# R times the state, for both scan directions, in one group over four quarters of the array

## The chip, the core and the metric

The kernel runs on one core of a Trainium2 chip. The metric is the device time of one launch in microseconds (us). Engines are named as in the profile: PE is TensorE's matmuls, PEld its weight loads, DVE VectorE, ACT ScalarE, POOL GpSimd, and SPq the queue of SyncE, which issues the DMAs.

## What is computed

A two-layer backbone over 1024 latent tokens and 256 context tokens of width 1024. Layer 0 mixes tokens with a bidirectional RWKV-7 scan, layer 1 with a Fourier transform; a squared-ReLU MLP follows each. What the change touches is the scan's output: per direction and head (16 heads of 64), a state S is carried through the tokens and read by r.

```
def step(s, inp):                                  # one token; inp = w, k, v, a, b, r
    sa = einsum('bhvk,bhk->bhv', s, a)
    s  = s * w[:, :, None, :] + sa[..., None] * b[:, :, None, :] + v[..., None] * k[:, :, None, :]
    y  = einsum('bhvk,bhk->bhv', s, r)
    return s, y
# for each direction: context tokens first (no y), then latent tokens from that state;
# direction 1 runs over the tokens in reverse
out = readout(y_direction0 + y_direction1)
```

## The kernel before

**Chunks.** The scan runs in 20 steps of 64 tokens (`scan_step`, line 912, called with i = 0 to 19): four context steps, then sixteen latent steps with outputs (`lat`). Each step handles a chunk of direction 0 and one of direction 1 (loop variable `d`). Within a chunk the recurrence is turned into matrix products, by head; a tile of 128 partitions holds two halves of 64 (`hh`), and `q` counts eight pairs of heads. `HR` names the two halves in order, `OR` the same two swapped.

**Products of one step.** Scores between the chunk's tokens (L957) go to banks 0 to 3 and give L (whose columns from `C` on hold r) and l2. `scan_invert` (line 1069) inverts the triangular part for both directions at once: L1147, L1160, L1183 and L1192 are 32-row products on TensorE, with transposes on VectorE between them; L1136 turns the keys. Then, for each direction, a chain: `x_mm` (L1014), a copy, `u_mm` (L1023), two copies of U into `sv`, and `s_mm` (L1037), which gives the next state. With outputs, `r_mm` (L1053) multiplies r with the state `st` and `y_mm` (L1059) adds l2 times `sv` in the same PSUM bank Y; ScalarE copies Y to `y` (L1065), and SP stores it to `s_y` (issued by the helper `dma`, L922). x, U, s and Y share three PSUM banks, 5 to 7 (`CHAIN`). In `r_mm` the half hh of L and of `st` lies on partitions `HR[hh]` and the output goes to partitions `HR[hh]` of Y, so one group uses the two quarters of 64x64 on the diagonal of the 128x128 array. The code's 16 float32 matmuls of a group stand as 32 rows in the profile.

**Rings.** Tiles come in turn from fixed places (`SCAN_RINGS`, line 278): six for L (three steps of two), three for `sv`, two each for `st`, `t` and `y`.

**The order.** Each operation is entered in a list (`plan.add`) with its engine, a planned duration, the keys it reads and writes, its bank and a `load` (how dense its TensorE work is counted). `Plan.emit` (line 165) then runs a list scheduler over all of it: it books each operation at its planned time, longest remaining path first, hands out banks and ring places, and writes the order of every engine's queue, SP's included, before anything runs. At run time each queue is strictly in its written order.

**Readout.** `readout` (line 1298) loads `s_y` of both directions by 128 tokens, adds them and goes on; the keys `("sy", d, chunk)` hold its loads (L1264) back until the stores are done. Behind it only matmuls with their epilogues follow: L368 to L370 are the three products in which a float32 product is split.

Of the kernel before, what the change touches and what calls it, by code (L numbers as in the profile page):

```python
# [22 lines left out]
CTX = 256  # L23
# [3 lines left out]
C = 64  # L27
# [264 lines left out]
SCORES, INVERT, CHAIN = range(4), (4,), range(5, 8)  # L292
# [38 lines left out]
class Kernel:  # L331
# [545 lines left out]
    def slot(self, name):  # L877
        k = self.count.get(name, 0)
        self.count[name] = k + 1
        ring = self.rings[name]  # L880
        return ring[k % len(ring)], (name, k % len(ring))
# [30 lines left out]
    def scan_step(self, i):  # L912
        nc, plan, slot = self.nc, self.plan, self.slot
        lat = i >= CTX // C
# [3 lines left out]
        HR = [slice(hh * 64, hh * 64 + 64) for hh in range(2)]  # L918
        OR = [HR[1], HR[0]]

        def dma(dst, src, kb, r=(), w=(), eng="q"):
            return plan.add(eng, min(1.3, kb / 200.0), lambda: nc.sync.dma_start(dst, src), r, w, hold=0.7)  # L922


        S = []
        for d in range(2):
            lo = i * C if d == 0 else (T + CTX - (i + 1) * C if lat else CTX - (i + 1) * C)
            c = 2 if not lat else (lo - CTX) // 512
            L, kL = slot("L")
            bk, kb = slot("bk")  # L930
            E = dict(lo=lo, c=c, L=L, kL=kL, bk=bk, kb=kb)
# [10 lines left out]
        for d in range(2):  # L942
            E = S[d]
            L, kL, bk, kb = E["L"], E["kL"], E["bk"], E["kb"]
            l2, k2 = slot("l2")
            bkt, kt_ = slot("bkt")
            E.update(l2=l2, k2=k2, bkt=bkt, kt=kt_)
            for h4 in range(2):
# [13 lines left out]
                for hh, B in enumerate(BB):  # L962
                    rs, ro = HR[hh], OR[hh]
                    bv = lambda B=B: B.tile.rearrange("p (q t) -> p q t", q=4)
                    ys = slice(d * 8 + q4.start, d * 8 + q4.stop)
# [18 lines left out]
        for d in range(2):  # L984
            E = S[d]
            sv, kv = slot("sv")
# [17 lines left out]
        for d in range(2):  # L1004
            E = S[d]
            L, kL, sv, kv = E["L"], E["kL"], E["sv"], E["kv"]
            lall = [(kL, "a", 0), (kL, "a", 1)] + [(kL, "k", hh, h4) for hh in range(2) for h4 in range(2)]
            vall = [(kv, z, hh) for z in ("s", "v") for hh in range(2)]
            B, U = self.plan.bank(CHAIN), self.plan.bank(CHAIN)

            def x_mm(B=B, L=L, sv=sv):
                for q in range(8):
                    for hh in range(2):
                        nc.tensor.matmul(B.tile[HR[hh], q * C : (q + 1) * C], L[hh][:, q, 0:C], sv[:, hh, q, :], start=True, stop=True)  # L1014

            self.at = plan.add("pe", 1.1, x_mm, lall + vall, [B], B, load=0.95)
            xs, kx = slot("xs")
            plan.flex({"act": 0.58}, lambda e, B=B, xs=xs: self.copy_on(e, xs, B.tile), [B], [kx], B)

            def u_mm(xs=xs, d=d, U=U):  # L1020
                for q in range(8):
                    for rs in HR:
                        nc.tensor.matmul(U.tile[rs, q * C : (q + 1) * C], tt[rs, d * 8 + q, :], xs[rs, q * C : (q + 1) * C],  # L1023
                                         start=True, stop=True)

            plan.add("pe", 1.1, u_mm, [kx, *kT], [U], U, load=0.5)
            for hh in range(2):
                plan.flex({"act": 0.58, "dve": 0.69}, lambda e, sv=sv, hh=hh, U=U: self.copy_on(
                    e, sv[HR[hh], hh].rearrange("p q c -> p (q c)"), U.tile[HR[hh]]), [U], [(kv, "s", hh)], U)
            if i < NCH - 1:  # L1030
                bkt, kt_ = E["bkt"], E["kt"]
                B = self.plan.bank(CHAIN)

                def s_mm(B=B, bkt=bkt, sv=sv):
                    for q in range(8):
                        for hh in range(2):
                            nc.tensor.matmul(B.tile[HR[hh], q * C : (q + 1) * C], bkt[:, hh, q, :], sv[:, hh, q, :],  # L1037
                                             start=True, stop=True)

                t, kt0 = slot("t")  # L1040
                plan.add("pe", 1.2, s_mm, vall + [(kt_, 0), (kt_, 1)], [B, kt0], B, load=0.78)
                self.state[d] = (t, kt0, [("pcs", d, kt, E["c"]) for kt in range(KT)])
                plan.add("dve", 0.68, lambda B=B, t=t, st=E["st"]: nc.vector.tensor_tensor(
                    t, B.tile.rearrange("p (q v) -> p q v", q=8), st, ALU.add), [B, E["ks"]], [kt0], B)
            if lat:
                l2, k2 = E["l2"], E["k2"]

                Y = self.plan.bank(CHAIN)

                def r_mm(B=Y, L=L, st=E["st"]):  # L1050
                    for q in range(8):
                        for hh in range(2):
                            nc.tensor.matmul(B.tile[HR[hh], q * C : (q + 1) * C], L[hh][HR[hh], q, C:], st[HR[hh], q, :],  # L1053
                                             start=q == 0, stop=False)

                def y_mm(B=Y, l2=l2, sv=sv):
                    for q in range(8):
                        for hh in range(2):
                            nc.tensor.matmul(B.tile[HR[hh], q * C : (q + 1) * C], l2[:, q, hh, :], sv[:, hh, q, :],  # L1059
                                             start=False, stop=q == 7)  # L1060

                plan.add("pe", 1.15, r_mm, vall + [E["ks"], (kL, "a", 0), (kL, "a", 1)], [Y], Y, load=0.5)
                plan.add("pe", 1.15, y_mm, vall + [(k2, hh, h4) for hh in range(2) for h4 in range(2)], [Y], Y, load=1.0)
                y, ky = slot("y")
                plan.add("act", 0.58, lambda B=Y, y=y: nc.scalar.copy(y, B.tile), [Y], [ky], Y)  # L1065
                dma(self.s_y[d, E["lo"] - CTX : E["lo"] - CTX + C].rearrange("t (h c) -> h t c", h=2), y, 256, [ky],
                    [("sy", d, (E["lo"] - CTX) // C)])

    def scan_invert(self, mab, kM, S):

# [227 lines left out]
    def readout(self):  # L1298
# [4 lines left out]
        def unit(t, qh):  # L1303

            ts_ = slice(t * P, (t + 1) * P)
            hq = lambda a: a.rearrange("p (h q c) -> p h q c", h=2, q=4)
            qv = lambda a: a.rearrange("p (q h c) -> p h q c", h=2, q=4)
            ys = [[("sy", d, 2 * t + z) for z in range(2)] for d in range(2)]
            y0, y1, v = [self.raw(src.rearrange("t (h x) -> t h x", h=2)[:, :, qh * 256 : qh * 256 + 256], 256,
                                  lambda t: t.rearrange("p (h x) -> p h x", h=2), r)  # L1310
                         for src, r in ((self.s_y[0, ts_], ys[0]), (self.s_y[1, ts_], ys[1]),
                                        (self.s_v[CTX + t * P : CTX + (t + 1) * P], [("v", qh, 2 + t)]))]
            m = self.M()
            plan.flex({"dve": 0.6, "pool": 1.24}, lambda e: self.engines[e].tensor_tensor(y0.tile, y0.tile, y1.tile, ALU.add),
                      [y1], [y0])
            plan.add("dve", 0.6, lambda: nc.vector.tensor_reduce(m.tile[:, 0:8], hv(y0.tile), AX.X, ALU.add), [y0], [m])
            plan.add("dve", 0.65, lambda: nc.vector.scalar_tensor_tensor(
                hv(y0.tile), bc(m.tile[:, 0:8]), -1.0 / C, hv(y0.tile), ALU.mult, ALU.add), [m], [y0])
            plan.add("act", 0.53, lambda: nc.scalar.activation(y1.tile, y0.tile, AF.Square), [y0], [y1])
            plan.add("dve", 0.6, lambda: nc.vector.tensor_reduce(m.tile[:, 8:16], hv(y1.tile), AX.X, ALU.add), [y1], [m])  # L1320
            plan.add("act", 0.25, lambda: nc.scalar.activation(
                m.tile[:, 16:24], m.tile[:, 8:16], AF.Sqrt, bias=self.eps[:, 1:2], scale=1.0 / C), (), [m])
            plan.add("dve", 0.1, lambda: nc.vector.reciprocal(m.tile[:, 24:32], m.tile[:, 16:24]), (), [m])
            ya, vb = self.S(), self.S()
            plan.flex({"dve": 0.6, "pool": 1.24}, lambda e: self.engines[e].tensor_tensor(
                qv(ya.tile[:, :512]), hq(y0.tile), m.tile[:, 24:32].rearrange("p (h q e) -> p h q e", h=2, e=1).broadcast_to(
                    [P, 2, 4, C]), ALU.mult), [y0, m], [ya])
            plan.flex({"dve": 0.6, "pool": 1.24}, lambda e: self.engines[e].tensor_tensor(
                qv(vb.tile[:, :512]), hq(v.tile), self.bon[:, t, qh * 8 : qh * 8 + 8].rearrange(
                    "p (q h e) -> p h q e", h=2, e=1).broadcast_to([P, 2, 4, C]), ALU.mult), [v, *[("bon", 4 * qh + k, t // 4) for k in range(4)]], [vb])  # L1330
            return ya, vb
# [631 lines left out]
```

## Time and profile before

| | |
|---|---|
| median of 3 runs | 3021.74 us (3017.54 to 3023.11) |
| profiled execution | 3018.24 us, its span 3016.5 us |
| mean granted clock of TensorE | 0.947 |
| TensorE busy (PE) | 2820.9 us, 94% of the span |
| weight loads (PEld) | 2187.5 us, 73% |
| VectorE busy | 1883.4 us, 62% |
| ScalarE busy | 997.1 us, 33% |
| GpSimd busy | 496.4 us, 16% |

A share is an average over the whole span, and stages differ; what a change in one stage is worth is read from that stage. "Idle before <-X" is time in which the engine stood still ahead of an instruction, put down to X, whose result came last; "issue" is idle time for which no wait shows. Matmuls overlap, so the start of one group and that of the next tell more than the length of one matmul.

### The profile page before, as it was taken

Reading aid. Unit: us, or ns where it says so; the run is one execution under the profiler, and the core shown is the slowest. Engines: PE = TensorE matmul, PEld = TensorE weight load, DVE = VectorE, ACT = ScalarE, POOL = GpSimd, SP = SyncE. Lnnn points to the kernel's source line nnn. Section 1 sums busy time; section 2 is a strip of 40 time slices with the busy share of each in tenths; the row PEclk is TensorE's granted clock in tenths of the full one; section 3 lists DMA queues with packets and bytes.
Section 4 is the critical chain, followed back from the end, with each engine's and each line's share of the span. In section 5 each row is a group of like instructions: output and inputs, shape, how many; then the busy total and the mean of one; then the engine's idle time right before and its main releaser. Section 6 shows DMA issues by size and latency. Waiting matters only on the chain.

```text
span 3016.5 us, 63005 instructions
## 1 busy us (share of the span) xinstructions
PE 2820.9 (94%) x26640; PEld 2187.5 (73%) x26640; DVE 1883.4 (62%) x3380; ACT 997.1 (33%) x1971; POOL 496.4 (16%) x425
## 2 busy tenths in 40 slices
PE   9999989988878878899999999999899999999998
PEld 5443446467777767788788888887797888888887
DVE  5398685537777777787565565446876454454455
ACT  4264454445555655342212111212332111111111
POOL 2064353300000000120101011101421011011110
PEclk9999989978888888899999999999799999999999
DMA  9266475633444454622332232111211111111111
GB/s 283 84 167 187 133 194 169 183 98 100 131 137 135 139 151 131 216 95 84 99 108 88 87 109 91 53 57 34 86 40 48 49 57 47 38 56 50 39 42 57
DMA packets 297291, 312.88 MB, mean 104 GB/s; under 512 B 81024, under 2 KB 212224, under 8 KB 297008
## 3 DMA queue, kind: packets, MB, share of 16 engines
q1 hardware_dynamic: 295648, 304.01, 33.5%
q0 software_dynamic: 1360, 4.84, 0.5%
q8 instruction: 209, 3.42, 0.5%
q14 instruction: 74, 0.61, 0.1%
HBM read 246.38 MB, written 62.39 MB: 102 GB/s over the span
## 4 chain that ended last, share of the span: by engine, by line
PE 70%; DVE 11%; issue 4%; DMA 3%; ACT 3%; POOL 0%; SPq 0%; DVEq 0%; ACTq 0%; POOLq 0%
PE ps L368 17%; PE ps L370 17%; PE ps L369 17%; PE ps L621 4%; PE ps L624 3%; PE ps L957 2%; PE ps L1037 1%; PE ps L1059 1%; PE ps L1023 1%; DVE bU L460 1%; PE ps L1160 1%; PE ps L1014 1%; DVE rU L1276 1%; PE ps L1147 1%; DVE bS L803 1%
## 5 line engine op out<-in xcount | busy, mean ns | idle before, releaser
L368 PE MATMUL ps<-rU,rU 128*128 128x512 f32 (+3 forms) x2632 | 979.9, 372 | 13.6 <-DVE rX L1546 8.0
L370 PE MATMUL ps<-rU,rU 128*128 128x512 f32 (+3 forms) x2632 | 976.5, 371 | 8.0 <-DVE rU L1276 5.3
L369 PE MATMUL ps<-rU,rU 128*128 128x512 f32 (+3 forms) x2632 | 975.4, 371 | 0.1
L368 PEld LDWEIGHTS ps<-rU,rU 128*128 128x128 f32 x2632 | 501.9, 191 | 107.5 <-DVE rX L1546 8.8
L370 PEld LDWEIGHTS ps<-rU,rU 128*128 128x128 f32 x2632 | 501.9, 191 | 99.8 <-DVE rU L1276 6.9
L369 PEld LDWEIGHTS ps<-rU,rU 128*128 128x128 f32 x2632 | 502.3, 191 | 90.1 <-DVE rU L1360 0.4
L1546 DVE SCALAR_TENSOR_TENSOR rX<-ps,mods,rX 128x512 f32<-128x512 f32 (+1 forms) x528 | 375.8, 730 | 123.6 <-PE ps L370 121.7
L1525 ACT ACTIVATE rS<-ps 128x512 f32<-128x512 f32 x122 | 73.1, 599 | 679.2 <-PE ps L370 678.5
L1276 POOL TENSOR_TENSOR rU<-rW,rU 128x512 fp32r<-128x512 f32 x74 | 118.7, 1609 | 1004.2 <-PE ps L370 519.1
L624 PE MATMUL ps<-bU,bU 128*128 128x512 f32 (+1 forms) x544 | 238.5, 575 | 1.2 <-ACT bX L427 0.9
L427 ACT CAST rU<-rW 128x512 fp32r<-128x512 f32 x161 | 97.2, 616 | 351.9 <-PE ps L370 255.6
L427 DVE CAST rU<-rW 128x512 fp32r<-128x512 f32 x115 | 55.2, 490 | 215.9 <-PE ps L369 210.0
L1276 DVE TENSOR_TENSOR rU<-rW,rU 128x512 fp32r<-128x512 f32 x200 | 173.2, 884 | 24.0 <-ACT rU L427 23.6
L427 DVE CAST rU<-rS 128x512 fp32r<-128x512 f32 (+1 forms) x97 | 45.0, 469 | 226.2 <-ACT rS L1528 198.9
L624 PEld LDWEIGHTS ps<-bU,bU 128*128 128x128 f32 x544 | 100.5, 193 | 107.5 <-issue 98.0
L621 PE MATMUL ps<-bU,bU 128*128 128x512 f32 x304 | 142.3, 609 | 0.0
L957 PE MATMUL ps<-sU,sX 64*128 64x128 f32 (+1 forms) x1280 | 121.9, 337 | 18.4 <-DVE sU L973 5.7
L957 PEld LDWEIGHTS ps<-sU,sX 64*128 64x128 f32 x1280 | 108.3, 240 | 28.0 <-issue 8.2
L427 ACT COPY sU<-ps 32x512 f32<-32x512 f32 (+2 forms) x186 | 96.0, 517 | 75.6 <-PE ps L1160 33.0
L1276 POOL TENSOR_TENSOR rU<-rS,rU 128x512 fp32r<-128x512 f32 x42 | 65.4, 1559 | 294.4 <-ACT rU L427 133.7
L621 PEld LDWEIGHTS ps<-bU,bU 128*128 128x128 f32 x304 | 56.5, 192 | 61.2 <-issue 57.6
L973 DVE TENSOR_TENSOR sU<-ps,sW 64x256 f32<-64x256 f32 x160 | 67.5, 422 | 50.1 <-ACT sX L966 20.4
(275 smaller groups left out, 3693.0 us busy)
## 6 DMA issues: line engine op xcount, KB each, us to landing
rW<-in_mlp_w_dram SPq DMA_DIRECT2D x256, 256.0 KB
rW<-in_k_mwt_dram SPq DMA_DIRECT2D x96, 256.0 KB
sX<-s_bk SPq DMA_DIRECT2D x40, 512.0 KB
s_ar<-bU SPq DMA_DIRECT2D x32, 512.0 KB
sU<-s_ar SPq DMA_DIRECT2D x64, 256.0 KB
sW<-in_k_mwt_dram SPq DMA_DIRECT2D x64, 256.0 KB
bU<-in_rk_wk_dram SPq DMA_DIRECT2D x48, 256.0 KB
bU<-in_rk_wv_dram SPq DMA_DIRECT2D x48, 256.0 KB
```

The source lines that it names most:

```text
L368: nc.tensor.matmul(out, w[0], x[0], start=start, stop=False)
L369: nc.tensor.matmul(out, w[0], x[1], start=False, stop=False)
L370: nc.tensor.matmul(out, w[1], x[0], start=False, stop=stop)
L427: self.nc.scalar.copy(out, src) if e == "act" else self.engines[e].tensor_copy(out, src)
L460: return self.plan.flex(durs, lambda e: self.engines[e].tensor_tensor(out, a, b, op), r, w)
L621: fn = lambda B=B, x=x, w=w, ms=ms, kt=kt: nc.tensor.matmul(B.tile, x[:, ms], w, start=kt == 0, stop=kt == KT - 1)
L624: fn = lambda B=B, x=x, w=w, ms=ms, kt=kt, n=n: nc.tensor.matmul(B.tile[:, :n], w[:, ms], x[:, :n], start=kt == 0, stop=kt == KT - 1)
L957: nc.tensor.matmul(BB[hh].tile[:, j * P : j * P + nr], bk[HR[hh], q, :], L[hh][HR[hh], q, :nr], start=True, stop=True)
L973: plan.add("dve", 0.41, lambda bv=bv, ro=ro, hh=hh, q4=q4, d=d, L=L: nc.vector.tensor_tensor(L[hh][ro, q4, 0:C], bv()[ro, :, 0:C], self.ma ...
L1276: plan.flex({"dve": n / 960 + 0.07, "pool": n / 440 + 0.08}, lambda e: self.engines[e].tensor_tensor(out(1), src(), f32(out(0)), ALU.subtr ...
L1525: plan.flex({"act": 0.53, "dve": 0.6}, lambda e, B=B, s=s: nc.scalar.activation(s.tile[:, :512], B.tile, AF.Relu) if e == "act" else nc.ve ...
L1546: plan.add("dve", n / 960 + 0.12, lambda B=B, m=m, n=n, xs=xs: nc.vector.scalar_tensor_tensor(xs(), B.tile[:, :n], self.mod(layer, 5, m), ...
```

## The change

For the sixteen steps with outputs, `r_mm` leaves the loop over directions. One `r_mm` now holds both directions' products, with direction and half alternating inside the loop over q; it waits for both directions' copies of U (`(kv, "s", hh)`), their states and their L tiles, takes two Y banks at once and is entered with 1.3 us and load 0.95 (before: 1.15 us and 0.5 for each direction). Direction 0's outputs stay on `HR[hh]`; direction 1's go to `OR[hh]`, the other half, so the four products in turn use all four quarters of 64x64. `y_mm` is entered behind it, once for each direction, and for direction 1 writes to the swapped halves as well. The copy to `y` is as before. Direction 1's store becomes two, one for each half, with a key each, and the readout's loads of direction 1 wait for both keys.

```diff
-            if lat:
-                l2, k2 = E["l2"], E["k2"]
-                Y = self.plan.bank(CHAIN)
-                def r_mm(B=Y, L=L, st=E["st"]):
-                    for q in range(8):
-                        for hh in range(2):
-                            nc.tensor.matmul(B.tile[HR[hh], q * C : (q + 1) * C], L[hh][HR[hh], q, C:], st[HR[hh], q, :],
-                                             start=q == 0, stop=False)
...
-                plan.add("pe", 1.15, r_mm, vall + [E["ks"], (kL, "a", 0), (kL, "a", 1)], [Y], Y, load=0.5)
-                plan.add("pe", 1.15, y_mm, vall + [(k2, hh, h4) for hh in range(2) for h4 in range(2)], [Y], Y, load=1.0)
...
+        if not lat:
+            return
+        Y = [self.plan.bank(CHAIN) for _ in range(2)]
+        YR = [HR, OR]
+        def r_mm():
+            for q in range(8):
+                for d in range(2):
+                    for hh in range(2):
+                        nc.tensor.matmul(Y[d].tile[YR[d][hh], q * C : (q + 1) * C], S[d]["L"][hh][HR[hh], q, C:], S[d]["st"][HR[hh], q, :],
+                                         start=q == 0, stop=False)
+        plan.add("pe", 1.3, r_mm, [k for E in S for k in ((E["kv"], "s", 0), (E["kv"], "s", 1), E["ks"], (E["kL"], "a", 0), (E["kL"], "a", 1))],
+                 Y, load=0.95)
+        for d in range(2):
+            E = S[d]
+            l2, k2, sv, kv = E["l2"], E["k2"], E["sv"], E["kv"]
+            def y_mm(B=Y[d], l2=l2, sv=sv, rows=YR[d]):
+                for q in range(8):
+                    for hh in range(2):
+                        nc.tensor.matmul(B.tile[rows[hh], q * C : (q + 1) * C], l2[:, q, hh, :], sv[:, hh, q, :],
+                                         start=False, stop=q == 7)
+            plan.add("pe", 1.15, y_mm, [(kv, z, hh) for z in "sv" for hh in range(2)] + [(k2, hh, h4) for hh in range(2) for h4 in range(2)],
+                     [Y[d]], Y[d], load=1.0)
+            y, ky = slot("y")
+            plan.add("act", 0.58, lambda B=Y[d], y=y: nc.scalar.copy(y, B.tile), [Y[d]], [ky], Y[d])
+            dst = self.s_y[d, E["lo"] - CTX : E["lo"] - CTX + C].rearrange("t (h c) -> h t c", h=2)
+            if d == 0:
+                dma(dst, y, 256, [ky], [("sy", d, (E["lo"] - CTX) // C)])
+            else:
+                for hh in range(2):
+                    dma(dst[hh], y[OR[hh]], 128, [ky], [("sy", d, (E["lo"] - CTX) // C, hh)])
```

In `readout`, `ys` becomes

```diff
-            ys = [[("sy", d, 2 * t + z) for z in range(2)] for d in range(2)]
+            ys = [[("sy", 0, 2 * t + z) for z in range(2)], [("sy", 1, 2 * t + z, hh) for z in range(2) for hh in range(2)]]
```

## Rows read from the trace of the kernel before

**Rows 1.** Stretches: us, busy us (instructions) of PE, PEld, DVE, ACT, POOL; clock, DMA share, GB/s

```profile
783.00:1234.00 451.00, 361.66 (x12046) 333.40 (x12040) 331.61 (x825) 253.77 (x556) 13.91 (x23) 0.85 0.48 143
1234.00:3016.00 1782.00, 1738.10 (x9101) 1450.50 (x9096) 1045.17 (x1755) 381.96 (x690) 245.53 (x179) 0.98 0.22 70
```

**Rows 2.** Costliest PE groups, 783 to 1240 us: busy us, mean ns | idle before, releasers

```profile
L1059 PE MATMUL ps<-sU,sU 128*64 128x64 f32 x1024 | 44.3, 249 | 5.9 <-issue 5.9
L1037 PE MATMUL ps<-sU,sU 128*64 128x64 f32 x960 | 44.3, 257 | 10.7 <-issue 10.7
...
L1053 PE MATMUL ps<-sU,sU 64*64 64x64 f32 x1024 | 36.5, 224 | 0.2 <-ACT sU L427 0.2
...
L1160 PE MATMUL ps<-sU,sU 32*32 32x32 f32 x1920 | 26.8, 213 | 15.4 <-issue 14.8 <-DVE sU L1152 0.6
```

**Rows 3.** The chain that ended last, 783 to 1240 us: shares, longest pieces (start, us)

```profile
by line: issue 11.4%; PE ps L957 9.7%; PE ps L1037 7.0%; PE ps L1059 6.5%; PE ps L1014 4.6%; PE ps L1160 4.2%; PE ps L1147 4.0%; PE ps L1023 3.9%; DVE sU L973 3.6%; ACT sU L427 3.4%; PE ps L1136 3.4%; PE ps L1053 3.2%; DVE sU L427 2.6%; DMA
...
1092.07 9.57 DMA sX<-s_bk
1118.99 10.48 DMA sU<-s_v
```

**Rows 4.** Timeline of PE, one step: start us, us, line, tiles, count [idle <-releaser]

```profile
803.30 1.15 PE L1014 MATMUL ps<-sU,sU 128*64 128x64 f32 x32
...
809.68 3.55 PE L1023 MATMUL ps<-sW,sU 64*64 64x64 f32 x64
813.16 0.77 PE L1147 MATMUL ps<-sU,sX 32*32 32x16 f32 x64
813.86 1.15 PE L1053 MATMUL ps<-sU,sU 64*64 64x64 f32 x32
814.93 1.34 PE L957 MATMUL ps<-sU,sX 64*128 64x128 f32 x16
816.21 1.15 PE L1053 MATMUL ps<-sU,sU 64*64 64x64 f32 x32
817.29 0.71 PE L1136 MATMUL ps<-ident,sX 64*128 64x64 f32 x16
817.92 1.15 PE L1037 MATMUL ps<-sU,sU 128*64 128x64 f32 x32
819.01 0.71 PE L1136 MATMUL ps<-ident,sX 64*128 64x64 f32 x16
819.64 1.15 PE L1059 MATMUL ps<-sU,sU 128*64 128x64 f32 x32
820.73 0.73 PE L1147 MATMUL ps<-sU,sX 32*32 32x16 f32 x64
821.43 1.15 PE L1037 MATMUL ps<-sU,sU 128*64 128x64 f32 x32
822.41 1.10 PE L1059 MATMUL ps<-sU,sU 128*64 128x64 f32 x32
823.55 0.31 PE L1160 MATMUL ps<-sU,sU 32*32 32x32 f32 x12
828.02 1.81 PE L1160 MATMUL ps<-sU,sU 32*32 32x32 f32 x116 [4.15 <-issue]
...
838.88 0.75 PE L1192 MATMUL ps<-sU,sX 32*32 32x32 f32 x64
```

**Rows 5.** SP's waits, 783 to 1240 us: line <- waited for: us, times, longest

```profile
SPq L922 <- PE ps L1053: 87.9, 22, 15.8
SPq L922 <- PE ps L1059: 52.3, 20, 5.8
```

**Rows 6.** The tile s_y: SP's issues of its stores, ns min/median/max, first and last start

```profile
L922 SPq DMA_DIRECT2D s_y<-sS x32: 514/535/608, 792.0 to 1240.8; - x32
```

**Rows 7.** DMA queues, 783 to 1240 us: packets, MB, share of 16 engines

```profile
q8 instruction: 95, 1.56, 1.4%
```

More of the change, by code (lines that the diff above doesn't have):

```diff
@@ L1044, in scan_step @@
                     t, B.tile.rearrange("p (q v) -> p q v", q=8), st, ALU.add), [B, E["ks"]], [kt0], B)
-            if lat:
-                l2, k2 = E["l2"], E["k2"]
-                Y = self.plan.bank(CHAIN)
-                def r_mm(B=Y, L=L, st=E["st"]):
-                    for q in range(8):
-                        for hh in range(2):
-                            nc.tensor.matmul(B.tile[HR[hh], q * C : (q + 1) * C], L[hh][HR[hh], q, C:], st[HR[hh], q, :],
-                                             start=q == 0, stop=False)
[L1056 to L1060, printed above, removed]
-                plan.add("pe", 1.15, r_mm, vall + [E["ks"], (kL, "a", 0), (kL, "a", 1)], [Y], Y, load=0.5)
-                plan.add("pe", 1.15, y_mm, vall + [(k2, hh, h4) for hh in range(2) for h4 in range(2)], [Y], Y, load=1.0)
[L1064 to L1067, printed above, removed]
```

## The prediction

> **What bounds the kernel now.** I read the stretches first: 783 to 1234 us are the sixteen scan steps that have outputs, and only there does the change act. TensorE is busy for 361.66 of these 451 us, VectorE for 331.61 and ScalarE for 253.77, so no engine is full; behind it, TensorE is busy for 1738.10 of 1782 us and bounds the kernel alone [rows 1]. What the scan gives up or takes therefore shifts the end nearly one to one, as the matmuls behind it begin when it hands over.
>
> Next the costliest TensorE groups of the scan [rows 2]. The products of R with the state (L1053) are 1024 matmuls and 36.5 us; each of the code's matmuls stands as two instructions, so a group of 16 is 32 rows and there are 32 groups, 1.14 us each. Their own idle time before them is 0.2 us: they are fillers, which wait for nothing. TensorE's longest idle times with one cause, 14.8 us ahead of L1160 and 10.7 ahead of L1037, are put down to "issue", which is no wait that a row shows.
>
> Then the chain of work that ended last over 783 to 1240 us [rows 3]. L1053 holds 3.2% of 457 us, 14.6 us; the other TensorE groups of its list hold 43.3% more, "issue" 11.4%, and two landings, of s_bk and s_v, hold 9.57 and 10.48 us. So R's groups are on the path for 14.6 of their 36.5 us, 40%, and in the rest they fill time that something else decides.
>
> Last the order of one step [rows 4]: u for both directions (L1023, x64), half of the next step's L1147, R of one direction, scores (L957), R of the other, then s (L1037) and y (L1059) by turns. And SP's queue: the issue helper's line L922 stands 87.9 us behind L1053, as the loads of a later step's L tiles need the tile that R reads last, and 52.3 us behind L1059 [rows 5].
>
> **The change, part by part.** *R's products in one group.* Removed are 32 groups at 1.14 us; added are 16 groups of 64 matmul rows that use four 64x64 quarters where each old group used the two on the diagonal. No row shows four quarters of this size at work. Bound above: they pair up only, 2 x 1.14 = 2.28 us a step, nothing saved (nothing lost either, as the same matmuls run in pairs today). Bound below: L1192, 64 matmuls over four tiles in 0.75 us [rows 4], though of 32 rows and columns. In between: an old group passes 16 matmuls through each of its two quarters in 1.15 us, 72 ns per matmul and quarter; if the four keep that pace side by side, 64 also take 1.15 us. I take 1.15, since it is the same shape at the same pace. It saves 2.28 - 1.15 = 1.13 us a step, 18.1 us of TensorE in 16 steps (bounds: 0, and 16 x 1.53 = 24.5).
>
> Whether quarters that share rows overlap is what decides between these. L1014's tiles share all 128 rows and alternate between the two column halves; 32 of them take 1.15 us, as long as L1053's 32 on the diagonal [rows 4], so sharing rows costs nothing that shows. The Trainium skill (TensorE: Matmul & The Clock Gate, section "Part 3: Packing small matmuls — row/col tiling") says that a weight load overlaps with matmuls in flight only when its row group differs. By that rule the two quarters over one row group would take turns, a group would stay near 2.28 us and this term would be 0. The trace disagrees for L1014, as far as equal times can say; I keep the rule as a rival.
>
> *What of it is on the path.* At the chain's share of 40%, 18.1 us give 7.2 us. Bounds: none of it (all filler) and all of it.
>
> *What is late next.* The profile's instruction queue moved 95 packets, 1.56 MB, in 457 us [rows 7], one per 4.8 us; with 12046 matmuls and 12040 weight loads in the scan [rows 1] that is some 253 instructions a packet. Half of a packet is one new group. The "issue" idles stand inside groups of one line, as at 828.02 after 12 of L1160's 128 [rows 4], so I read them as TensorE waiting for its own instructions. Faster R work asks for the next packet 1.13 us earlier, and where a packet is late already the saving turns into "issue". In the step shown the stop comes eight groups and 10.7 us after R's second group, so I take nothing off here, and the whole 7.2 in a rival below. The Trainium skill (Runtime: NRT & Kernel Launch, section "Instruction fetch mechanics") has fetches in blocks of 16 KiB or 256 instructions, which agrees with 1.56 MB over 95; it calls the cost of crossing into a block mostly hidden, which the idle before L1160 does not bear out. By it, too, nothing would come off.
>
> *The joint wait.* The group needs both directions' copies of U, and two of the three banks 5 to 7 at once, held until both outputs are copied. The first direction's R can no longer fill the time in which the second's copies run: about 2.35 us lay between the two old starts, 813.86 and 816.21. Behind it on TensorE's queue stand both y groups, and on SP's the loads of L. The scores and turns that lie between (L957, L1136) can fill the same place, so I price it at 0; uncovered it is one old group in every step, 16 x 1.14 = 18.2 us, the bound, and the other end is a gain of nothing.
>
> *Outputs with swapped lanes.* The second direction's y products keep number and shape (128x64, 64 columns), and the copy on ScalarE its length; cost 0, with L1059's idle of 5.9 us, all "issue", as the bound on what order could give or take there. Its store becomes two, so SP issues 16 more at 0.535 us [rows 6], 8.6 us in all, hidden by the 140.2 us in which SP stands behind L1053 and L1059; uncovered they cost those 8.6. Bytes stay. Only the last one is seen, by the readout that loads it: +0.5 us. Readout's longer key lists issue nothing.
>
> *The new order.* The order is written from planned times, with one entry at 1.3 in place of two at 1.15, so everything behind the first of these steps can move, waits on landings among it. I price that at 0; one landing more or less on the path is worth about 10 us [rows 3].
>
> Sum: -7.2 + 0.5 = -6.7 us. The profiled execution took 3018.24 us, its span 3016.5 and 1.7 around it; the sum gives 3011.5 there. It ran 3.5 us under the median of 3021.74, and on that median I predict 3015.0.
>
> **The rivals.** *All of it counts.* In the scan TensorE is busy or in "issue" most of the time, and a list-made order can give every freed slot to waiting work. Then 18.1 - 0.5 = 17.6 us go: 3004.1. For it: 80% busy. Against: 40% on the chain.
>
> *Nothing arrives.* Either the quarters only pair up (2.28 us a step), or the saving stands as "issue" before L1160, L1037 or L1147. For it: 11.4% of the chain is "issue" already. Against: eight groups between R and the next stop in the step shown. The time is +0.5: 3022.2. It covers also a group that runs as said beside work that decides anyway.
>
> *Slower: the joint group holds SP.* L tiles come free when R has read them. If the group starts only after the second direction's copies and after s has given up its banks, the first direction's tile comes free later than now, SP stands longer at the load of L, and behind it in order stand the loads of s_bk and s_v, whose landings already hold 9.57 and 10.48 us of the path. Two more such pieces cost 20.0: 3015.0 + 20.0 = 3035.0. It decides from the point at which the load behind R lands after the scores group that reads it could start. For it: 87.9 us of SP behind L1053, its greatest wait. Against: L has six tiles, three steps of two, so loads run well ahead.
>
> **How the numbers follow.** The forecast has 0.45, with its own range of 3007 to 3023 (most of one landing, 8 of its 10 us, either way); all of it 0.15; nothing 0.18; slower 0.22. Runs of this kernel tell about 0.2%, 6.0 us, from no change. Beyond it on the fast side lie 0.27 of the forecast's chance and all of the first rival: 0.42. Within it lie 0.18 and 0.18: 0.36. Slower: 0.22. The range takes in the first rival at 3004 and, on the other side, one and a half landings above the forecast, 3030 and a little over, as the slower rival may come with less than its two: 3003 to 3031.
>
> **What would show it.** In the changed trace the R line should have 1024 matmuls in 16 groups at about 1.15 us, 18 to 19 us busy; 36 us would show that the quarters don't overlap. The step should shrink by about 0.4 us, with the scan's end some 7 us earlier and the matmul stretch behind it as long as now. More "issue" by the amount saved shows the second rival; SP's wait behind the R line above 88 us, with more landings on the chain, the third. The prediction is wrong if the R line falls as said and the scan's end does not move, or moves by more than 15 us either way.

## The result: slower by 0.44%

The changed kernel took 3032.67 us (median of 20 runs, 3021.08 to 3038.68) against 3017.91 us for the kernel before in the same comparison (20 runs, 3011.38 to 3029.26): a ratio of 1.0044, 95% interval 1.0035 to 1.0054, or +14.8 us where 6.7 less were forecast. Two executions of it were profiled, at 3023.66 and (run e11 below) 3027.38 us, in the lower half of its runs; so rows explain 5 to 9 us directly, and the rest of the median by repetition only.

The changed kernel has other line numbers: R is L1055 (L1053 before), y L1067 (L1059), Y's copy L1073 (L1065), and L1159, L1172 and L1148 are the former L1147, L1160 and L1136. Stretches of the changed kernel, columns as in [rows 1]:

```profile
783.00:1234.00 451.00, 351.47 (x11809) 320.91 (x11810) 328.02 (x807) 256.22 (x562) 11.70 (x19) 0.85 0.51 146
1234.00:3016.00 1782.00, 1742.86 (x9169) 1455.57 (x9167) 1044.64 (x1761) 379.17 (x685) 243.99 (x178) 0.99 0.22 69
```

TensorE is busy 10.2 us less in the scan, at the same granted clock of 0.85, a mix of the two levels. Its groups there, as in [rows 2]:

```profile
L1067 PE MATMUL ps<-sU,sU 128*64 128x64 f32 x992 | 40.8, 243 | 8.7 <-issue 8.7
...
L1037 PE MATMUL ps<-sU,sU 128*64 128x64 f32 x928 | 40.0, 242 | 13.0 <-issue 8.4 <-ACT sU L427 2.1 <-DVE sU L1043 1.3
...
L1172 PE MATMUL ps<-sU,sU 32*32 32x32 f32 x1920 | 28.7, 218 | 26.8 <-issue 26.0 <-DVE sU L1164 0.8
...
L1055 PE MATMUL ps<-sU,sU 64*64 64x64 f32 x960 | 20.9, 231 | 1.0 <-DVE sU L427 0.9
```

R fell from 36.5 us to 20.9 for the 15 groups that lie behind 783 us, so 22.3 for 16. The joint wait, 0.9 us on VectorE's copy of U (2.5 us with the first group, which runs before 783 us), is nearly all that stands before it. "Issue" ahead of L1172 grew from 14.8 to 26.0. One step of TensorE's timeline, as [rows 4]:

```profile
864.10 1.15 PE L1037 MATMUL ps<-sU,sU 128*64 128x64 f32 x32
865.18 0.27 PE L1148 MATMUL ps<-ident,sX 64*128 64x64 f32 x1
865.75 0.68 PE L1148 MATMUL ps<-ident,sX 64*128 64x64 f32 x15 [0.30 <-DVE sU L978]
866.36 0.33 PE L1055 MATMUL ps<-sU,sU 64*64 64x64 f32 x4
866.97 1.15 PE L1055 MATMUL ps<-sU,sU 64*64 64x64 f32 x60 [0.27 <-DVE sU L427]
868.04 0.73 PE L1159 MATMUL ps<-sU,sX 32*32 32x16 f32 x64
```

Sixty rows over four quarters take 1.15 us, what 32 rows over two took: the quarters overlap. The Trainium skill (TensorE: Matmul & The Clock Gate, section "Part 3: Packing small matmuls — row/col tiling") says that a weight load overlaps with matmuls in flight only when its row group differs, by which the two quarters over one row group would take turns. The trace disagrees with this rule for tiles of 64 by 64, as 64 rows by turns would take an estimated 2.3 us, twice 1.15.

The loss stands behind the scan. Below are the last y group, the filler (products with ident that only fill waits) and the first matmul that spreads the norm (L1453, now L1465), in the kernel before and then in the changed one:

```profile
1232.09 2.08 PE L1059 MATMUL ps<-sU,sU 128*64 128x64 f32 x64
...
1241.93 3.53 PE L1851 MATMUL ps<-ident 128*128 128x128 f32 x24
...
1249.00 8.65 PE L1851 MATMUL ps<-ident 128*128 128x128 f32 x76
...
1340.38 1.06 PE L1453 MATMUL ps<-rS,spot 128*128 128x128 f32 x8
```

```profile
1222.27 2.08 PE L1067 MATMUL ps<-sU,sU 128*64 128x64 f32 x64
...
1230.04 16.24 PE L1863 MATMUL ps<-ident 128*128 128x128 f32 x144
...
1255.05 8.65 PE L1863 MATMUL ps<-ident 128*128 128x128 f32 x76
...
1345.03 1.05 PE L1465 MATMUL ps<-rS,spot 128*128 128x128 f32 x8
```

The last y group ends 9.8 us sooner (1224.4 against 1234.2), the norm starts 4.7 us later. From here on "handover" is the stretch between these two: 106.2 us before, 120.7 after. What follows the norm is as long as before (1676.9 us against 1676.1). The lead of 9.8 us was there long before the scan's end: in the second of the sixteen output steps, u (809.68 us in [rows 4]) starts 10.1 us sooner in the changed kernel,

```profile
799.54 2.42 PE L1023 MATMUL ps<-sW,sU 64*64 64x64 f32 x64
```

and from there to the start of the last y group both kernels take the same, 422.4 us before and 422.7 after. So the later output steps did not get shorter.

In the handover a run of 144 filler rows, 16.24 us, has taken the place of 24 rows. It covers a wait for the readout, whose loads are on SP's queue. SP's issues in the changed kernel, and then in the kernel before:

```profile
1229.78 0.87 SPq L1276 DMA_DIRECT2D rW<-s_y  x1
1230.75 0.96 SPq L1276 DMA_DIRECT2D rW<-s_v  x1
1231.80 2.69 SPq L897 DMA_DIRECT2D sW<-in_k_mwt_dram  x3
1240.57 1.74 SPq L1276 DMA_DIRECT2D rW<-s_y  x2
1242.40 0.56 SPq L1276 DMA_DIRECT2D rW<-s_v  x1
1243.06 15.71 SPq L1276 DMA_DIRECT2D rW<-in_rk_wo_dram  x8
```

```profile
1229.14 1.41 SPq L1264 DMA_DIRECT2D rW<-s_y  x2
1231.94 0.52 SPq L1264 DMA_DIRECT2D rW<-s_v  x1
1232.51 0.59 SPq L1264 DMA_DIRECT2D rW<-s_hg  x1
1233.15 1.52 SPq L1338 DMA_DIRECT2D rX<-in_k_xt_dram  x3
...
1240.32 0.40 SPq L1264 DMA_DIRECT2D rW<-in_rk_wo_dram  x1
```

In the changed kernel three loads of in_k_mwt stand among the readout's loads. They feed the rows of mod_w: 64 side products that VectorE does in the scan when it has time (L898), with four places of their own, W0 to W3, which the readout's loads take over (rW). Behind these three SP stands still until 1240.57, when a place comes free: first 2.2 us for a store of s_y to land, then 3.8 us for a row. SP's waits for rows, 1225 to 1250 us (columns as in [rows 5]), and VectorE's timeline there:

```profile
SPq L1276 <- DVE sW L898: 5.5, 4, 3.8
```

```profile
1238.07 0.69 DVE L1326 TENSOR_TENSOR rW<-rW,rW 128x512 f32<-128x512 f32 x1 [3.94 <-DMA rW<-s_y]
...
1239.55 0.98 DVE L898 SCALAR_TENSOR_TENSOR sW<-sW,sF 128x512 f32<-128x512 f32 x1
```

The row stands in VectorE's order behind a sum of the readout (L1326) that waits 3.94 us for a landing, and the readout's next loads wait for the row: each holds the other up in turn. The instructions on L898 after 1200 us, in the kernel before and in the changed one (count, ns, first and last start):

```profile
L898 DVE SCALAR_TENSOR_TENSOR sW<-sW,sF x4: 655/678/693, 1202.0 to 1216.1; 128x512 f32<-128x512 f32 x4
```

```profile
L898 DVE SCALAR_TENSOR_TENSOR sW<-sW,sF x16: 639/682/985, 1200.9 to 1242.9; 128x512 f32<-128x512 f32 x16
```

In VectorE's order 23 of the 64 now stand behind the first step of the last inversion, against 8 before; these are called late from here on. SP's waits, as [rows 5], in the changed kernel and, for the one line not shown there, in the kernel before:

```profile
SPq L897 <- DVE sW L898: 78.8, 23, 14.2
SPq L922 <- PE ps L1067: 56.6, 26, 8.8
SPq L922 <- PE ps L1055: 44.1, 11, 7.8
```

```profile
SPq L897 <- DVE sW L898: 41.4, 15, 14.6
```

SP's wait behind R is half of what it was (87.9), that behind the rows nearly double. The chain over 783 to 1240 us ends, beside "issue" at 16.5% (11.4% in [rows 3]), in a landing of s_y. Its load was issued ahead of the three loads above; the chain comes to it from a row that ran at 1228.50:

```profile
by line: issue 16.5%; PE ps L957 11.9%; PE ps L1067 6.8%; PE ps L1014 6.4%; PE ps L1172 5.8%; PE ps L1037 5.5%; ACT sU L427 4.5%; PE ps L1159 3.6%; DMA rW<-s_y 3.6%; PE ps L1023 3.3%; DVE sU L973 3.3%; PE ps L1148 3.1%; DVE sU L427 2.9%; PE
...
1229.78 8.27 DMA rW<-s_y
```

### The profile page after: what moved, and what is told of

It reads as the page before. It is cut to its first block, busy times and chain, and to the rows that moved or that the text cites. A ratio compares the mean times of both kernels' runs of the same rounds, so it can differ in the third digit from the quotient of the medians.

```text
span 3021.9 us, 63296 instructions
## 1 busy us (share of the span) xinstructions
PE 2813.3 (93%) x26776; PEld 2179.2 (72%) x26776; DVE 1883.8 (62%) x3378; ACT 998.8 (33%) x1977; POOL 493.0 (16%) x421
## 4 chain that ended last, share of the span: by engine, by line
PE 75%; DVE 11%; issue 6%; ACT 4%; DMA 3%; POOL 1%; SPq 0%; DVEq 0%; ACTq 0%; POOLq 0%
PE ps L368 17%; PE ps L370 17%; PE ps L369 17%; PE ps L624 6%; PE ps L621 4%; PE ps L957 3%; DVE bU L460 1%; PE ps L578 1%; PE ps L1172 1%; PE ps L1037 1%; PE ps L1014 1%; PE ps L1067 1%; ACT sU L427 1%; PE ps L1023 1%; DMA rW<-s_y 1%
## 5 line engine op out<-in xcount | busy, mean ns | idle before, releaser
L957 PEld LDWEIGHTS ps<-sU,sX 64*128 64x128 f32 x1280 | 110.5, 246 | 18.4 <-DVE sU L973 5.9
```

What stands on the lines that cost most here:

```text
L957: nc.tensor.matmul(BB[hh].tile[:, j * P : j * P + nr], bk[HR[hh], q, :], L[hh][HR[hh], q, :nr], start=True, stop=True)
```

## The experiments

Four theories. A: the group of four quarters pays, and the loss is made at the handover by the rows of mod_w that the new order lays late. B: what the faster group saves is waited away in the scan. C: the joint group's waits, or the lanes and stores, cost. D: each written order has its own luck of some 10 us. Ratios are against the kernel before.

**e1, joint group in pairs.** The change with both directions on the diagonal, so its written order row for row, but without the quarters:

```
-        YR = [HR, OR]
+        YR = [HR, HR]
```

> The changed kernel with direction 1's outputs left on their own half, so that the joint group uses two quarters and not four; its written order is that of the changed kernel, row for row, and its two stores stay. Theory A (the four quarters pay in the scan, and the loss is made later, by mod_w rows that the new order lays at the scan's end): a group goes from about 1.2 to 2.28 us, the scan grows by 7 to 17 us, about 3040 us in all. Theory B (the faster group brings nothing, its saving is waited away in the scan): as the changed kernel, 3033. Theory C (the joint wait and the stores are what costs): 3033 too, as both stay.

3031.52 us, 1.0047 (1.0031 to 1.0063): as the change. Stretch, R and L1172 of e1:

```profile
783.00:1234.00 451.00, 351.77 (x11927) 322.40 (x11924) 327.28 (x808) 258.39 (x566) 11.75 (x19) 0.88 0.52 146
```

```profile
L1055 PE MATMUL ps<-sU,sU 64*64 64x64 f32 x960 | 32.5, 220 | 2.2 <-DVE sU L427 2.1
...
L1172 PE MATMUL ps<-sU,sU 32*32 32x32 f32 x1920 | 27.0, 211 | 28.5 <-issue 25.7 <-DVE sU L1164 2.9
```

The quarters save 11.6 us of R (32.5 against 20.9), yet TensorE's busy time is equal: all its other groups took 319.3 us here and 330.6 in the change, at a granted clock of 0.88 against 0.85. Its last y group ends at 1229.0. The "issue" before L1172 is there without the quarters too. B for the saving; the loss is no matter of the quarters. (With the quarters e1 also gives up the swapped lanes of direction 1's y; it keeps the two stores.)

**e2, lanes and stores alone.** The kernel before with the second direction's lanes swapped and its store in two:

```
+                rows = [HR, OR][d]
...
-                            nc.tensor.matmul(B.tile[HR[hh], q * C : (q + 1) * C], ...
+                            nc.tensor.matmul(B.tile[rows[hh], q * C : (q + 1) * C], ...
...
+                    for hh in range(2):
+                        dma(dst[hh], y[OR[hh]], 128, [ky], ...
```

> The kernel before with swapped lanes and two stores for direction 1 alone; R's groups stay two, of two quarters each. Theory A: the mod_w rows stay where they were (9 behind the last step's inversion against 8 before and 23 in the changed kernel), so 3018 within 6 us. Theory C (16 more stores on SP's queue, and the readout's longer wait for them): 3026 or more.

3009.69 us, 0.9970 (0.9955 to 0.9984): faster by 0.3%, and below the 3018 within 6 us that A expected. C falls for lanes and stores.

**e3, the group booked as the two that it replaces.**

```
-        plan.add("pe", 1.3, r_mm, ... load=0.95)
+        plan.add("pe", 2.3, r_mm, ... load=0.5)
```

> The changed kernel with the joint group booked in the list at 2.3 us and load 0.5, as the two old groups together were; what runs is the same. 7 mod_w rows are then laid behind the last inversion, against 23. Theory A: the scan keeps its 7 to 10 us and the readout starts with it, about 3010. Theory B: 3018, as before. Theory C: 3030, as the joint wait and the stores stay.

3025.89 us, 1.0019 (1.0006 to 1.0032): half of the loss is gone, with 7 rows late. No theory's figure fits, and its handover is 116.4 us, nearly that of the change, though no more rows are late than in the kernel before.

**e4, the rows ranked first.** The change with

```
+                    plan.rank = 100.0
                     self.mod_part(...)
```

> The changed kernel, its group booked as in the change, with the scan's mod_w rows given a higher rank in the list, so that 4 of 64 stand behind the last inversion in place of 23. Theory A: 3010 to 3018; the rows delay the scan a little, but no longer the readout. Theories B and C: 3030, as nothing of the group or its stores changes.

3030.97 us, 1.0034 (1.0018 to 1.0049), as B and C expected and not A. Four rows are late and the handover is 105.8 us, but the scan ends 26 us later than in the change: either the loss moved, or the late rows did not make it.

**e5 and e6, the order of before kept.** e6 has the old order with swapped lanes and the second store laid right behind the first; e5 moves the first R group, in 12 of 16 steps, to the place of the second and joins them. In 7 of these 12 steps something that reads or overwrites the operands stands between the two places, so that some of its products are formed from a later step's tiles.

```
-                self.pair[i] = z[0][1], False
+                self.pair[i] = z[0][1], z[0][0] == z[1][0] == "r"
```

> The kernel before in its own written order, kept row for row, but where R's two groups of a step have no y group between them (12 of 16 steps) both are issued in one group of four quarters at the place of the later one; lanes swapped, direction 1's store in two at the place of the one. Theory D (the group itself does no harm, and the order that the list writes for it is what costs): at most 3018, and 3006 if the 12 x 1.03 us of TensorE were all on the path; 3013 with the chain's 40%. Theory C (the joint group as such costs): over 3025. Theory B (what the group saves is waited away or lost to the clock): 3018, as its twin e6.

> The same written order, lanes and stores as e5, with R's groups left as two of two quarters: the twin of e5. It differs from the kernel before by swapped lanes and a second store at the place of the first alone. All theories: 3018 within 4 us; if stores cost, 3022 or more. e5 less e6 is what the four quarters give by themselves in this order.

e5 3026.53 us, 1.0030 (1.0013 to 1.0046); e6 3006.62 us, 0.9971 (0.9955 to 0.9986), the fastest here that computes all, where all theories expected 3018 within 4 us. Lanes and stores gain again. e5 lies 20 us over its twin, in the range of C, but its group stood 18.9 us behind landings of s_ar, the loads of L tiles:

```profile
L1061 PE MATMUL ps<-sU,sU 64*64 64x64 f32 x960 | 28.4, 253 | 19.9 <-DMA sU<-s_ar 18.9 <-ACT sU L435 0.9
```

The change's group has no such wait (its row above), so e5 does not price the joining.

**e7 and e8, another order for each.** One weight of the planner, in the kernel before and in the change:

```
-REST_DEAR, REST_WEIGH = {"pool": 1.3, "dve": 1.276}, {"dve": 1.195}
+REST_DEAR, REST_WEIGH = {"pool": 1.3, "dve": 1.276}, {"dve": 1.25}
```

> The kernel before with the list's weight for VectorE in the scan and behind it at 1.25 in place of 1.195: another written order of the same work. Theory D (each order has its own luck of some 10 us, and the one before was a good one): anywhere in 3010 to 3035. Theory C: it stays under e8 by about 13 us.

> The changed kernel with the same weight of 1.25. Theory D: anywhere in 3010 to 3035, and its distance to e7 has nothing to do with the 14 us between the two kernels of the case. Theory C: some 13 us over e7.

3025.68 us, 1.0027 (1.0011 to 1.0043), and 3045.88 us, 1.0093 (1.0072 to 1.0114). D holds to this extent: the weight alone moves the kernel before by 8 us and the changed one by 13. The change is 20 above its twin here too, with 26 rows late in e8 and 6 in e7; e8 lies outside D's range, and the distance speaks for C or A.

**e9 and e10, no rows at all.** The scan without its mod_part calls:

```
-                    self.mod_part(0, 16 + (i - 3) % 8 * 4 + j, (i - 3) // 8, lambda w=w: w, kw, [self.at])
```

> The kernel before without the 64 rows of mod_w that VectorE multiplies and sums in the scan (L898) and their loads; mods 16 to 47 are then mod_b alone (that part of the computation is left out). It is the twin of the next run. What the rows themselves cost: in the kernel before VectorE is busy 49 us with them, mostly beside waits, so all theories expect this kernel at or below the kernel before: 2995 to 3018 us.

> The changed kernel without the same 64 rows and loads, so that nothing of theirs can be laid behind the last inversion and hold the places that the readout's loads want. Theory A (the loss is made at the handover by these rows, the group of four quarters pays in the scan): the filler ahead of the readout shrinks to about 4 us, the stretch from the last y group to the first norm matmul is as long as in its twin, and the kernel is 0 to 10 us below its twin. Theory C (the joint group's waits cost wherever they fall): 10 to 20 us above its twin. Theory D (each written order has its own luck): anything within 12 us of it.

3014.84 us, 0.9994 (0.9983 to 1.0006), and 2982.87 us, 0.9896 (0.9879 to 0.9914). Without the rows the changed kernel falls by 50 us, the one before by 3. The direction is A's; the size is beyond each theory, and the handover is not as long as the twin's but 33 us shorter (82 against 115). The twin's, without any row, is itself longer than the 106.2 of the kernel before.

**e11, the change again.**

> The changed kernel again, for a second profile at its usual time. If the loss at the handover belongs to the written order, the stretch behind the last y group is again about 120 us (106 in the profile of before) and the run of filler ahead of the readout's first loads about 16 us; the 9 us by which the first profile lies below the median of its runs are then in the scan, with more of it at the lower clock.

3027.38 us. Its last y group ends at 1231.0 and its norm starts at 1348.6, a handover of 117.6 us with the same 144 rows of filler (16.24 us): the loss there belongs to the order. The scan ended 6.6 us later than in the first profile, at a clock of 0.84.

**e12, a joint group in five steps, nothing else moved.** e6, with R joined only where no user of its operands stands between:

```
+                after = [spot[q] for q in ops[r[0][2]]["suc"]]
+                self.pair[i] = r[0][1], min(after) > spot[r[1][2]]
```

> The order of e6_kept_split, instruction for instruction, except that the first direction's R group is moved to the place of the second's and joined with it in those 5 of the 16 steps where nothing that reads or overwrites its operands stands between the two. So each of the 5 joint groups saves about 0.9 us of TensorE, and nothing else moves. Against e6_kept_split (3006.6): theory B or 'the quarters pay': 2 to 5 us below, 3002 to 3005. Theory C (a joint wait costs about 1 us each or more): 3 to 10 us above, 3010 to 3017. A result within 2 us says that five joint groups neither pay nor cost what can be measured.

3008.74 us, 0.9972 (0.9960 to 0.9985): as e6 (0.9971). Five joint groups neither pay nor cost what these runs can tell; of sixteen in this order nothing is known.

**e13 and e14, the late rows moved forward.** The change with a higher rank for the rows of its last steps, 30 in e13 and 100 in e14:

```
+                    plan.rank = 30.0 if i >= 13 else 0.0
                     self.mod_part(...)
+                    plan.rank = 0.0
```

> The changed kernel with the rows of mod_w of steps 13 to 18 ranked 30 higher. In the written order all is as in the changed kernel up to the 18th inversion; 15 of the 23 rows that it lays behind the last inversion are laid ahead of it, so 8 stay late, as in the kernel before. Theory A (the late rows hold the places that the readout's loads want): the stretch from the last y group to the first norm matmul falls from 118 to 121 us to 100 to 108, the scan grows by 0 to 6 (15 rows of 0.76 us on VectorE in its last step), sum 3017 to 3027, 6 to 15 below the changed kernel's 3032.7. Theory C (the joint group's own waits cost): the handover moves and the time stays at 3030 to 3036. Theory D: 3020 to 3040 with no relation to the handover.

> As e13 with a rank of 100: none of the rows stands behind the last inversion, 28 of them stand between the 19th and the last one. Theory A: the handover as in e13 or shorter (96 to 106 us), but 28 rows of 0.76 us (21 us of VectorE) now stand ahead of the last inversion's own VectorE work, so the scan may grow by 0 to 15: 3012 to 3032. Theory C: 3030 to 3045.

e13 took 3014.97 us, 0.9995 (0.9980 to 1.0009): the loss is gone, and the time lies a little below A's range of 3017 to 3027. Its handover, by the rows below, is 91.2 us, and SP loads s_y and s_v without a row's load between; but the scan ends at 1249.2, later by 24.9 us than in the change and not by the 0 to 6 expected. e14 took 3036.73 us, 1.0055 (1.0039 to 1.0072), outside A's range and inside C's: its handover is 10.2 us shorter than the change's (110.5), but with 28 rows in one inversion its scan ends 29 us later.

```profile
1245.74 3.49 PE L1069 MATMUL ps<-sU,sU 128*64 128x64 f32 x64
...
1251.07 8.42 PE L1865 MATMUL ps<-ident 128*128 128x128 f32 x74
...
1340.41 1.05 PE L1467 MATMUL ps<-rS,spot 128*128 128x128 f32 x8
```

**e15 and e16, e2 and e1 without the rows**, by the edit of e9.

> e2_lanes (groups of R kept apart, second direction's lanes swapped, two stores) without the 64 rows of mod_w (mods 16 to 47 are mod_b alone). If the 32 us of e10 below its twin belong to the lanes and stores: 2980 to 2990. If they belong to the joint group: 3000 to 3015, as e9 (3014.8) or as e2 below it.

> e1_pairs (one joint group in the same place of the order as the change, but its rows in pairs of quarters, so about 2.0 us and not 1.1) without the 64 rows. Its written order is that of e10, so: if the quarters' 0.9 us per step pay once the handover does not eat them, it lies 6 to 14 us above e10 (2989 to 2997); if the scan waits them away (theory B), within 3 us of e10 (2980 to 2986); if the order of the joint group has nothing to do with the 32 us, near e9 (3010 to 3018).

3007.45 us, 0.9962 (0.9946 to 0.9979), and 2985.60 us, 0.9887 (0.9870 to 0.9905). With e10 at 0.9896 (0.9879 to 0.9914), quarters and pairs are again equal, and the gain without rows belongs to the joint group's order. Stretch and R (L1054) of e10, then of e16:

```profile
783.00:1234.00 451.00, 357.03 (x12167) 326.65 (x12164) 327.27 (x734) 265.79 (x584) 26.05 (x31) 0.87 0.45 125
...
L1054 PE MATMUL ps<-sU,sU 64*64 64x64 f32 x1024 | 22.0, 232 | 6.0 <-DVE sU L427 3.9 <-ACT sU L427 2.1
```

```profile
783.00:1234.00 451.00, 359.64 (x11841) 329.87 (x11842) 319.58 (x718) 262.22 (x574) 25.40 (x30) 0.88 0.44 124
...
L1054 PE MATMUL ps<-sU,sU 64*64 64x64 f32 x960 | 34.4, 229 | 5.6 <-DVE sU L427 3.6 <-ACT sU L427 2.1
```

R differs by 12.4 us (16 groups in e10's window, 15 in e16's), the busy time by 2.6, and the last y group ends at 1230.0 and 1229.3.

**e17 and e18, the rows on other engines.** In the change and in e2, GpSimd multiplies and ScalarE sums:

```
+            self.plan.add("pool", 1.24, lambda: nc.gpsimd.tensor_tensor(w(), w(), self.silr, ALU.mult), ...
+            self.plan.add("act", 0.6, lambda: nc.scalar.activation(w(), w(), AF.Copy, accum_out=...
```

> The changed kernel with the 64 rows of mod_w multiplied on GpSimd and summed by ScalarE, so that none of them stands in VectorE's written order and none is late. Theory A (late rows make the loss): the time comes near that of the changed kernel without the rows (2982.9): 2983 to 3003, with 80 to 100 us from the last y group to the first norm matmul. Theory C or D: 3015 to 3035, as the changed kernel. GpSimd's product may take 1.2 us or more beside VectorE; 64 of them are 80 us or more in a scan of 460 in which GpSimd is busy 12, so they should stay off the path.

> e2_lanes (groups kept apart, lanes swapped, two stores) with its rows on GpSimd and ScalarE in the same way. Its rows were not in the way (e15 without them 3007.5, e2 with them 3009.7), so theory A expects 3000 to 3010, and e17 below it by 5 to 25 us, as e10 lay 24.6 below e15. If e17 is not below it, the 24.6 us of the pair without rows came from leaving the rows out of that order and not from the joint group.

e17 took 3016.57 us, 0.9998 (0.9983 to 1.0014), e18 3012.77 us, 0.9979 (0.9964 to 0.9995). The group on GpSimd, and e17's last y group and first spread:

```profile
L899 POOL TENSOR_TENSOR sW<-sW,sF 128x512 f32<-128x512 f32 x64 | 81.1, 1292 | 88.9 <-DMA sW<-in_k_mwt_dram 65.0 <-DVE sS L1123 17.6 <-DVE sF L890 6.0
```

```profile
1232.92 2.08 PE L1072 MATMUL ps<-sU,sU 128*64 128x64 f32 x64
...
1337.18 1.05 PE L1470 MATMUL ps<-rS,spot 128*128 128x128 f32 x8
```

With all outputs kept and no row in VectorE's order the change's loss of 15 us is gone, and the handover is 102.2 us; four rows still run late, on GpSimd. But the time does not reach the range of A (2983 to 3003) and lies in that of C and D (3015 to 3035), and e17 does not lie below e18: by the expectation's own words, the 24.6 us between e15 and e10 came from leaving the rows out of that order, not from the joint group.

## Why the prediction was wrong, by its steps

*The new order* is the step that failed: "I price that at 0", and with it the sentence that the matmul stretch behind the scan stays "as long as now". That stretch grew from 1782.3 to 1797.5 us, and nearly all of the growth lies in the handover, 14.5 us (11.4 in e11). That the written order makes the loss is shown by leaving out the rest: e1 has this order and the same loss without the quarters, e2 and e6 have the lanes and stores and no loss, the joint wait is 2.5 us in all, and in e10, e16 and e17 sixteen joint groups run without the loss.

What in this order makes it is in part argued. For the late rows speak the trace, in which the order laid 15 more of them late, their loads stand among the readout's and SP stands 3.8 us for one of them, and e13 and e17, which take them out of the handover in different ways and each lose the whole 0.44%. Against the twins with the same lanes and stores, the order with the joint group costs 23.0 us with the rows on VectorE (e2), 3.8 with them on GpSimd (e18), less than the runs can tell, and gains 24.6 without them (e15). Against it speak e3, e4 and e14, which also leave no more rows late than the kernel before, and keep half of the loss, most of it, and more than all of it. A long handover comes without them too: 116.4 us in e3, 115.5 in e9, some 5 us of which is later work that these orders lay ahead of the norm. And in e13 the handover is 29.5 us shorter than in the change, the scan's end 24.9 later: the profiles account for 4.6 of the 17.7 us between the two medians. So the loss hangs on these rows and the order around them; that it is the late ones is supported, not shown.

*What of it is on the path*, -7.2 us: this term was near nothing. Two pairs differ in the quarters and the lanes that go with them: e1 against the change, 1.0047 and 1.0044, and e16 against e10, 0.9887 and 0.9896, 2.7 us at most. The share of the chain told where R stood, not what its going would free; the other groups took the time again, at a lower granted clock. Whether the clock fell because of the shorter group was not tried. The scan's end did come sooner by 9.8 and 3.2 us, around the 6.7 of the sum, but e1's came 5.2 us sooner without the quarters, and the first profile's lead stood already at the second of the sixteen output steps: the number was right by luck. "The step should shrink by about 0.4 us" failed with it, and so did the reading that the change acts in the output steps only.

*R's products in one group*: the mechanism was right, 1.15 us for a group at the upper level; the saving in busy time was 14.2 us (36.5 - 22.3) and not 18.1, as some groups ran at the lower level or waited inside.

*The joint wait*, priced at 0 with 18.2 as its bound: 0.9 us for 15 groups and 2.5 for all (3.0 and 6.6 in e11). Right in the main, and e12 agrees for five groups.

*Outputs with swapped lanes*, priced at 0 with 8.6 as its bound: the tile's stores became 47 in the window at a median of 0.539 us, and together with the lanes they are no cost but a gain of 8 to 11 us in e2 and e6, and of 7 in e15 against e9. Why is open.

```profile
L922 SPq DMA_DIRECT2D s_y<-sS x47: 460/539/1623, 797.9 to 1229.1; - x47
```

*What is late next*: "issue" rose as the second rival says, but in e1, which saves nothing in R, as much; so it came with the order. That it is TensorE waiting for its own instructions no run here shows.

*The rivals.* The slower one had the right sign and nearly the time (3035.0), and an engine that the trace bears out, SP. Its place was wrong: it looked for SP behind R, where the wait fell from 87.9 to 44.1 us; that its time came so near is luck. The quarters did not "only pair up"; that nothing of their saving arrives was the other half of the second rival, and this half held.

## What to carry to other kernels

Where an order is written from planned times, an edit's own price is the smaller part: before pricing the rest at nothing, list the work that the planner lays wherever it finds slack, and ask which of it can slide into the next stage and which places and queue it holds there. A filler's saved time need not be worth its share of the chain; here nothing of it showed. To price one part, keep the order fixed and change that part alone (e1, e6, e12). To convict or clear a suspect, move it in several ways and count the moves that do not help too: each move writes a new order, and here an order alone was worth 8 to 13 us.

## What the runs showed of the hardware

Four 64x64 quarters at work give 60 rows in 1.15 us, where 32 rows over two quarters took 1.15; pairs in the same place took 32.5 us for 15 groups where quarters took 20.9. That 11 to 12 us less of R's products in 451 us shorten nothing, with a granted clock of 0.85 against 0.88 and 0.87 against 0.88, was not expected; nor that two half stores in place of one, with swapped lanes, go with a gain of 8 to 11 us, nor that one order without 64 side rows is 50 us faster where another gains 3. None of these three has a cause shown here.
